# A hybrid decoder layer on Trainium2: in the first token block, norms and low parts in another order, a third projection begun early, weights divided a step ahead, and eight stores put off

## The chip, the cores and the metric

The kernel runs on one core of a Trainium2 chip. The metric is the device time of one execution in microseconds (us), and of several runs the median. A profile is one further execution, recorded by the hardware profiler. The engines are named as in the profile: PE (TensorE, matmuls and transposes), DVE (VectorE), ACT (ScalarE), POOL (GpSimd) and SP (SyncE, which issues nearly all DMA transfers here). Each engine works through its own instructions in a fixed order, and waits where an input or a buffer is not ready.

## The reference

One decoder layer over 16 meta tokens and 2048 real tokens of width 1024, in float32. Cut to what matters here:

```python
def reference(x, meta_tokens, ...):
    h = layer_norm(concatenate([meta, x], axis=1), ln_in_g, ln_in_b)
    mix = hybrid_mixer(h, w_in, b_in, ...)
    h = layer_norm(ALPHA * h + mix, ln1_g, ln1_b)
    h = layer_norm(ALPHA * h + swiglu(h), ln2_g, ln2_b)
    return h[:, N_META:]

def hybrid_mixer(h, w_in, b_in, ...):
    proj = einsum('bld,de->ble', h, w_in) + b_in
    q_s, k_s, v_s, q_g, k_g, v_g, r_g, g_lr = split(proj, cuts, axis=-1)
    o_s = sliding_window_gqa(q_s, k_s, v_s, sinks)
    o_g = chunked_gla(q_g, k_g, v_g, log_g)
    ...
    return einsum('ble,ed->bld', concatenate([o_s, o_g], axis=-1), w_out)
```

## The kernel before

**Precision.** A float32 product is made of three matmuls in a shorter format: a tile is divided into a high part (a copy on ACT, line 185) and a low part (tile minus high part, on DVE or POOL, line 186), and high x high, high x low and low x high are summed. Weights are divided once, stored to DRAM in divided form (line 226, 1024 KB each) and loaded back for later blocks (line 220).

**Tiling.** The 2048 tokens go in four blocks of 512 (`TB`), each of four tiles of 128 tokens. For each block, tokens are loaded and normalised, transposed on PE and divided into `h` (two tiles of eight 128-wide slices of the width, four each), and then multiplied by "units", blocks of 128 columns of the input projection. Unit 0 holds the window attention's keys, unit 1 its values, 2 to 5 its queries, 6 to 9 queries and keys of the gated linear attention. `project` makes one unit of one block: 24 matmuls (8 slices, 3 terms) into a PSUM bank `pu`. The first two units of the first block are begun with the first 256 tokens alone (`begin`, half-width matmuls) and finished in `project`.

**The first block.** `first_tokens` writes its order out by hand: `bank_stats`, `total`, `mean`, `square`, `variance`, `centre` and `scale` make the norm of a tile (with the power of the variance on POOL, line 422), `turn(n)` transposes tile n and divides it, `parts(u)` divides unit u. What is wrapped in `held` stays in program order on its engine. All else (matmuls of `begin`, DMA) is placed by a scheduler, which orders each engine's instructions by its own costs; so are the four blocks' further steps, listed in `WINDOW_STEPS`. `turn` also stores the divided transposed tokens to DRAM (`hT_sc`, line 461, 512 KB each, two for each tile, eight in the block), which a later stage reads.

**Buffers that set the order.** `st_u`, the staging of a unit's weights, has three buffers; `hl_u`, the divided unit, four; units 0 and 1 keep theirs until the meta tokens have been multiplied by them (`project_meta`, small matmuls `pm`). `pu` has two banks for all but the third unit. In the trace `x` is a tile of tokens, `tp` a transposed one, `kr` and `khh`/`kll` the keys, `vn`, `vd`, `vl` the values and their parts, `qraw` and `qs` queries, `s` scores, `lr` the power of a variance. Each DMA of SP also waits for the landing of the one eight places ahead of it.

**After the first block** the same steps go on for blocks 1 to 3 (divided units loaded back), then come the linear attention, the output projection and the feed-forward part.

Of the kernel before, what the change touches and what calls it, by code (L numbers as in the profile page):

```python
# [14 lines left out]
P = 128  # L15
D = 1024
KT = D // P
# [106 lines left out]
def body(ctx, tc, t, seq):  # L124
    nc = tc.nc
# [65 lines left out]

    hm = cp.tile([P, 2, KT, NM], F32R, name="hm")

    def matmuls(out, terms):
        n = len(terms)
        for i, (l, r) in enumerate(terms):
            nc.tensor.matmul(out, l, r, start=(i == 0), stop=(i == n - 1))  # L197

    rows = [slice(0, 64), slice(64, 128)]
    kTm = cp.tile([P, 2, NM], F32, name="kTm")  # L200
# [6 lines left out]
    def fetch(src, name):  # L207
        w = src.shape[1] * src.shape[2]
        st = staging(f"st_{name}")[:, :w]
        nc.sync.dma_start(st, src.rearrange("p k c -> p (k c)"))  # L210
        return st

    divided = {}

    def unit(src, name, c=P, lo_eng=None, st=None, key=None, hold=lambda i: i):

        n = src.shape[1] * src.shape[2]
        hl = wpool.tile([P, 2, D], F32R, tag="whl", name=f"hl_{name}", bufs=4)[:, :, :n]
        if key in divided:
            nc.sync.dma_start(r32(hl), divided[key])  # L220
        else:
            if st is None:
                st = fetch(src, name)
            split_into(hl[:, 0, :], hl[:, 1, :], st, lo_eng or nc.gpsimd, hold)
            divided[key] = dr.tile([P, 2, n], F32, name=f"w_{name}")
            nc.sync.dma_start(divided[key], r32(hl))
        return hl.rearrange("p a (k c) -> p a k c", c=c)


# [5 lines left out]
    def at(h, a, k):  # L235

        return h[k // 4][:, a, k % 4]
# [36 lines left out]
    with ExitStack() as c1:  # L274
# [24 lines left out]
        fetched = [fetch(t["w_u"][0], "u0_0")]  # L299
        first.append(wp.tile([P, D], F32, tag="pr", name="x_last", bufs=2))  # L300
        held(nc.sync.dma_start(first[3], t["x"][3 * P : 4 * P, :]))
        fetched.append(fetch(t["w_u"][1], "u1_0"))
        xm = wp.tile([P, D], F32, tag="pr", name="xm", bufs=2)
        nc.sync.dma_start(xm[:NM], t["meta"])
        lnt = mconst("lnt", [P, 2, KT], t["ln_in_t"])
# [86 lines left out]
            for g in range(2):  # L392
                anchor[:] = [nc.sync.dma_start(hT_sc[s][:, :, 4 * g : 4 * g + 4, q], r32(h[g])[:, :, :, q])]

        anchor = []

        def first_tokens(h):

# [27 lines left out]
            def total(n):  # L426
                sums[n] = lsmall(f"sm_{n}", [P, 1])
                held(nc.scalar.activation(junk, first[n], AF.Copy, accum_out=sums[n]))

            def mean(n):  # L430
                m[n] = lsmall(f"lm_{n}", [P, 1])
                held(nc.vector.tensor_scalar(m[n], sums[n], -1.0 / D, None, op0=ALU.mult))
# [5 lines left out]
            def variance(n):  # L438
                v[n] = lsmall(f"lv_{n}", [P, 1])
                held(nc.vector.tensor_scalar(v[n], squares[n], 1.0 / D, EPS_LN, op0=ALU.mult, op1=ALU.add))  # L440
                power(n)

            def centre(n):
                held(nc.vector.scalar_tensor_tensor(first[n], first[n], m[n], lng, op0=ALU.subtract if n == 0 else ALU.add, op1=ALU.mult))

            def scale(n):
                for g in range(2):
                    w = slice(512 * g, 512 * g + 512)
                    held(nc.vector.scalar_tensor_tensor(first[n][:, w], first[n][:, w], r[n], lnb[:, w], op0=ALU.mult, op1=ALU.add))
                nc.sync.dma_start(h_sc[n * P : n * P + P, :], first[n])  # L450

            def turn(n):
                q = slice(n * P, n * P + P)
                for g in range(2):
                    tp = t_psum(f"tp{n}_{g}") if n % 2 else s_psum(f"tp{n}_{g}").rearrange("p (k q) -> p k q", q=P)
                    for j in range(4):
                        k = 4 * g + j
                        nc.tensor.transpose(tp[:, j, :], first[n][:, k * P : (k + 1) * P], ident)
                    split_into(h[g][:, 0, :, q], h[g][:, 1, :, q], tp, None, held)
                for g in range(2):  # L460
                    stored[n] = nc.sync.dma_start(hT_sc[0][:, :, 4 * g : 4 * g + 4, q], r32(h[g])[:, :, :, q])

            w = {}

# [15 lines left out]
            turn(0)  # L480
            parts(0)
            square(2)
            centre(2)
            variance(2)
            scale(2)
            turn(1)
            begin(0, h, w[0])
            total(3)
            mean(3)
            square(3)  # L490
            centre(3)
            variance(3)
            parts(1)
            scale(3)
            turn(2)
            begin(1, h, w[1])
            turn(3)
            return stored[1], small_constants()

        halves = slice(0, TB // 2), slice(TB // 2, TB)  # L500
        EARLY_UNITS = 2
        begun = {}

        def begin(u, h, w):

            pt = mm_psum(f"pu{u}_0") if u < 2 else ps.tile([P, 512], F32, tag="L", name=f"pu{u}_0", bufs=1)
            c = halves[0]
            matmuls(pt[:, c], [m for k in range(KT) for m in ((w[:, 0, k, :], at(h, 0, k)[:, c]), (w[:, 0, k, :], at(h, 1, k)[:, c]), (w[:, 1, k, :], at(h, 0, k)[:, c]))])
            begun[u, 0] = w, pt

        def project(u, s, h, want_meta=False):
            w, pt = begun.pop((u, s), None) or (unit(t["w_u"][u], f"u{u}_{s}", P, nc.vector if (u, s) == (2, 0) else None, key=u), mm_psum(f"pu{u}_{s}"))
            terms = lambda a, b: [m for k in range(KT) for m in ((w[:, 0, k, :], a(k)), (w[:, 0, k, :], b(k)), (w[:, 1, k, :], a(k)))]
            c = halves[1] if s == 0 and u < EARLY_UNITS else slice(0, TB)
            matmuls(pt[:, c], terms(lambda k: at(h, 0, k)[:, c], lambda k: at(h, 1, k)[:, c]))
            if want_meta:
                metas[u] = w
            return pt
# [180 lines left out]
        for s in range(NSB):  # L699
            if s == NSB - 2:  # L700
                with behind(anchor):
                    tri, head, bvg, gng, eye, lev, w2, brh, brg = gla_constants()
            if s + 1 < NSB:
                hid[s + 1] = hidden(s + 1)
            for what in WINDOW_STEPS.split():
                op, k = what[0], int(what[1])
                if op == "q":
                    qs[s, k] = swa_q(s, k, hid[s])
                elif op == "S":
                    swa_scores(s, k, {c: qs.get((s, c)) for c in range(4)})  # L710
                elif op == "V":
                    swa_values(s, k)
                elif op == "G":
                    gla_qk(s, k, hid[s])
                elif s + 1 < NSB:
                    if op == "L":
                        with behind(ends if (s, k) == (0, 0) else ()):
                            load_tokens(s + 1, hid[s + 1], k)
                    elif op == "K":
                        (swa_keys, swa_vals)[k](s + 1, hid[s + 1])  # L720
                    else:
                        qs[s + 1, k] = swa_q(s + 1, k, hid[s + 1])

# [1003 lines left out]
```

## Time and profile before

| | |
|---|---|
| runs | 2231.46, 2235.39, 2230.97 us; median 2231.46 |
| the profiled execution | 2232.63 us |
| its span, first to last instruction | 2230.4 us |
| instructions | 31502 |
| mean granted clock of PE | 0.99 |
| read from and written to DRAM | 306.67 and 152.17 MB |

A row of the timeline gives start and duration in us, engine, line, operation, output and inputs, shapes and the number of merged instructions, and in brackets how long the engine had been idle and who ended that. A row of the windows gives, for each engine in turn, the us it was busy with the number of instructions, then PE's granted clock, the busy share of the DMA engines, and GB/s. A row of waits gives who waited for whom, the us in total, how often, and the longest. The page's slices are 40 equal parts of the span, with the busy share in tenths.

### The profile page before, as it was taken

What the parts mean: (1) busy time and instruction counts of PE and PEld (TensorE: products, weight loads), DVE (VectorE), ACT (ScalarE), POOL (GpSimd) and SP (SyncE); (2) the same over time, 40 slices, a digit from 0 to 9 for tenths busy, and PEclk for the clock granted to TensorE, in tenths of its full rate; (3) what the DMA queues carried; (4) which work ended last, traced back from release to release, by engine and by line L of the source; (5) the groups of instructions that cost most, each with busy time, mean ns of one, the idle gap of its engine ahead of it and who ended that gap; (6) DMA issues with size and microseconds to landing.
All of it is one profiled execution on the core that took longest, in us unless ns stands there. A gap on an engine that the chain in (4) does not pass through costs nothing.

```text
span 2230.4 us, 31502 instructions
## 1 busy us (share of the span) xinstructions
PE 2164.5 (97%) x11540; PEld 1861.3 (83%) x11540; DVE 1432.3 (64%) x2285; ACT 838.2 (38%) x1477; POOL 1219.7 (55%) x951
## 2 busy tenths in 40 slices
PE   7999999999999999999999999999999999999998
PEld 5888889888989988878888888788888888888886
DVE  6666554565745567367998666765657555865687
ACT  5555554635352343342222223222322242232343
POOL 4766545745624162258776756766666536432433
PEclk9999999999999999999999999999999999999999
DMA  9969673666676686766444317523232299655563
GB/s 328 338 225 286 226 260 114 230 258 242 239 252 262 223 319 222 297 227 223 159 166 142 112 62 259 210 85 128 81 132 81 95 345 330 216 198 170 165 232 128
DMA packets 181918, 460.92 MB, mean 207 GB/s; under 512 B 16978, under 2 KB 65011, under 8 KB 167684
## 3 DMA queue, kind: packets, MB, share of 16 engines
q1 hardware_dynamic: 176804, 452.26, 58.0%
q10 hardware_dynamic: 4960, 6.65, 0.8%
q8 instruction: 91, 1.49, 0.3%
q14 instruction: 63, 0.52, 0.1%
HBM read 306.67 MB, written 152.17 MB: 206 GB/s over the span
## 4 chain that ended last, share of the span: by engine, by line
PE 84%; DVE 6%; DMA 5%; issue 2%; POOL 2%; ACT 2%; SPq 0%; DVEq 0%; POOLq 0%; ACTq 0%
PE t L197 21%; PE d L1360 17%; PE b L197 15%; PE pu L197 11%; PE po L197 7%; PE pv L197 4%; PE lp L1134 2%; PE oa L667 2%; DMA cb<-n_scT 1%; DMA x<-x 1%; PE s L614 1%; PE s L615 1%; DMA gg<-mG_sc 1%; PE pt L655 1%; PE op L1154 1%
## 5 line engine op out<-in xcount | busy, mean ns | idle before, releaser
L1360 PE MATMUL d<-B,A 128*128 128x512 f32 x1848 | 419.3, 389 | 0.4 <-DVE A L186 0.4
L1360 PEld LDWEIGHTS d<-B,A 128*128 128x128 f32 x1848 | 346.8, 188 | 72.8 <-DVE A L186 0.8
L197 PE MATMUL t<-h_t,ps 128*128 128x512 f32 x1584 | 368.1, 390 | 5.1 <-DMA ps<-parts_ps 2.5
L197 PEld LDWEIGHTS t<-h_t,ps 128*128 128x128 f32 x1584 | 296.7, 188 | 68.1 <-ACT ps L185 2.8
L197 PE MATMUL pu<-h,hl_u 128*128 128x512 f32 (+1 forms) x1008 | 246.1, 390 | 6.4 <-ACT hl_u L185 3.3
L197 PE MATMUL b<-h_b,pa 128*128 128x512 f32 x1032 | 241.7, 389 | 0.6 <-DMA pa<-parts_pa 0.6
L197 PEld LDWEIGHTS b<-h_b,pa 128*128 128x128 f32 x1032 | 193.5, 188 | 41.2 <-issue 1.0
L186 POOL TENSOR_TENSOR pa<-a,pa 128x1024 fp32r<-128x1024 f32 x62 | 162.0, 2614 | 100.7 <-ACT pa L185 100.7
L197 PEld LDWEIGHTS pu<-h,hl_u 128*128 128x128 f32 x1008 | 180.4, 193 | 39.0 <-ACT hl_u L185 3.7
L197 PE MATMUL po<-hl_o,msh 128*128 128x256 f32 x1024 | 199.8, 291 | 3.0 <-DVE yo L913 1.5
L186 DVE TENSOR_TENSOR A<-rA,A 128x1024 fp32r<-128x1024 f32 (+1 forms) x78 | 118.8, 1549 | 122.2 <-ACT A L185 122.2
L197 PEld LDWEIGHTS po<-hl_o,msh 128*128 128x128 f32 x1024 | 164.1, 194 | 4.4 <-DVE yo L913 2.1
L185 ACT ACTIVATE A<-rA 128x1024 fp32r<-128x1024 f32 (+1 forms) x78 | 78.6, 1042 | 213.3 <-PE d L1360 199.5
L197 PE MATMUL po<-hl_o,msl 128*128 128x256 f32 x512 | 147.4, 288 | 0.0
L1630 DVE TENSOR_TENSOR u<-u,t 128x512 f32<-128x512 f32 x132 | 89.6, 681 | 82.7 <-PE t L197 82.5
L197 PE MATMUL b<-h_b,ps 128*128 128x512 f32 x528 | 125.4, 393 | 3.1 <-ACT h_b L185 2.8
L197 PE MATMUL t<-h_t,pa 128*128 128x512 f32 x528 | 123.8, 389 | 0.0
L1556 POOL TENSOR_TENSOR a<-a,a 128x1024 f32<-128x1024 f32 x42 | 121.3, 2887 | 1.6
L197 PEld LDWEIGHTS b<-h_b,ps 128*128 128x128 f32 x528 | 99.7, 189 | 25.1 <-ACT h_b L185 3.2
L197 PEld LDWEIGHTS t<-h_t,pa 128*128 128x128 f32 x528 | 99.0, 188 | 20.4
L185 ACT ACTIVATE ps<-a 128x1024 fp32r<-128x1024 f32 x63 | 66.7, 1058 | 116.6 <-PE t L197 74.8
L186 DVE TENSOR_TENSOR ps<-a,ps 128x1024 fp32r<-128x1024 f32 x42 | 77.1, 1836 | 50.2 <-ACT ps L185 47.8
(355 smaller groups left out, 4281.0 us busy)
## 6 DMA issues: line engine op xcount, KB each, us to landing
hl_u<-w_u SPq DMA_DIRECT2D x42, 1024.0 KB, 6.5
a<-w_gu SPq DMA_DIRECT2D x84, 512.0 KB, 4.7
rA<-a_sc SPq DMA_DIRECT2D x66, 512.0 KB, 4.6
w<-w_d SPq DMA_DIRECT2D x50, 512.0 KB, 5.4
hl_o<-w_o SPq DMA_DIRECT2D x24, 1024.0 KB, 7.2
hT_sc<-h SPq DMA_DIRECT2D x32, 512.0 KB, 6.6
gh<-hT_sc SPq DMA_DIRECT2D x16, 1024.0 KB, 9.6
w_u<-hl_u SPq DMA_DIRECT2D x14, 1024.0 KB, 8.3
```

The source lines that it names most:

```text
L185: hold(nc.scalar.activation(hi, src, AF.Copy))
L186: hold((lo_eng or nc.vector).tensor_tensor(lo, src, r32(hi), op=ALU.subtract))
L197: nc.tensor.matmul(out, l, r, start=(i == 0), stop=(i == n - 1))
L614: nc.tensor.matmul(sp[:, :272], q, khh[:, hh, w], start=True, stop=False)
L615: nc.tensor.matmul(sp[:, :272], q, kll[:, hh, w], start=False, stop=True)
L655: nc.tensor.transpose(tp[:, x, :], pr[:, n, 2 * (x % 2) + x // 2, NM:144], ident)
L667: nc.tensor.matmul(oa[:, n], l, m, start=False, stop=(hh == 1 and i == 5))
L1134: nc.tensor.matmul(o[:, P * j : P * j + P], kl[:, j, :], x[:, :, j, :], start=True, stop=True)
L1154: nc.tensor.matmul(op[:, P * h : P * h + P], am[:, h, :], vg[n][:, 16 + P * h : 16 + P * h + P], start=False, stop=(h % 2 == 1))
L1360: nc.tensor.matmul(pt, a_[:, a, ca], fb[:, b, cb], start=(p == 0 and j == 0), stop=(p == NP - 1 and j == 2))
L1556: sub = lambda o, x, y: nc.gpsimd.tensor_tensor(o, x, y, op=ALU.subtract)
L1630: nc.vector.tensor_tensor(o[i], x[i], y[i], op=ALU.add)
```

## The change

- The low parts of a token tile are placed directly behind its high parts: tile 1 is turned ahead of the centring of tile 2, and unit 1's parts come ahead of the square of tile 3.
- A third unit is fetched at the start, divided in `first_tokens` and begun with the first 256 tokens (in another PSUM tile, `L`); its second half is 24 half-width matmuls in `project`. The matmuls of the begun units' second halves are kept in program order.
- Weights are divided a step ahead: at the end of `project` of a unit of the first block, the next unit's division is begun (`ahead`, order in `FIRST_UNITS`).
- The eight stores of `hT_sc` for the first block are collected (`put_off`) and issued at the end of the block's steps, behind the store of the last divided unit.

```diff
-    def matmuls(out, terms):
+    def matmuls(out, terms, hold=lambda i: i):
...
-            nc.tensor.matmul(out, l, r, start=(i == 0), stop=(i == n - 1))
+            last = hold(nc.tensor.matmul(out, l, r, start=(i == 0), stop=(i == n - 1)))
+        return last
...
-            nc.sync.dma_start(divided[key], r32(hl))
+            stored_parts.append(nc.sync.dma_start(divided[key], r32(hl)))
...
-        fetched.append(fetch(t["w_u"][1], "u1_0"))
+        fetched += [fetch(t["w_u"][u], f"u{u}_0") for u in (1, 2)]
...
-                    stored[n] = nc.sync.dma_start(hT_sc[0][:, :, 4 * g : 4 * g + 4, q], r32(h[g])[:, :, :, q])
+                    put_off.append((hT_sc[0][:, :, 4 * g : 4 * g + 4, q], r32(h[g])[:, :, :, q]))
...
             turn(0)
             parts(0)
             square(2)
-            centre(2)
-            variance(2)
-            scale(2)
             turn(1)
             begin(0, h, w[0])
             total(3)
+            centre(2)
+            variance(2)
             mean(3)
+            parts(1)
             square(3)
+            scale(2)
+            begin(1, h, w[1])
+            variance(3)
             centre(3)
-            variance(3)
-            parts(1)
             scale(3)
             turn(2)
-            begin(1, h, w[1])
+            parts(2)
             turn(3)
+            begin(2, h, w[2])
+            ahead(3, 0, held)
...
-        EARLY_UNITS = 2
+        EARLY_UNITS = 3
...
+        FIRST_UNITS = [3, 6, 5, 4, 9, 8, 7]
+        units_ahead = {}
+
+        def ahead(u, s, hold=lambda i: i):
+            units_ahead[u, s] = unit(t["w_u"][u], f"u{u}_{s}", P, None, key=u, hold=hold)
...
-            w, pt = begun.pop((u, s), None) or (unit(t["w_u"][u], f"u{u}_{s}", P, nc.vector if (u, s) == (2, 0) else None, key=u), mm_psum(f"pu{u}_{s}"))
+            w, pt = begun.pop((u, s), None) or (units_ahead.pop((u, s), None) or unit(t["w_u"][u], f"u{u}_{s}", P, None, key=u), mm_psum(f"pu{u}_{s}"))
...
+            if s == 0 and u in FIRST_UNITS[:-1]:
+                ahead(FIRST_UNITS[FIRST_UNITS.index(u) + 1], 0)
...
+            if s == 0:
+                with behind(stored_parts[-1:]):
+                    for o, x in put_off:
+                        nc.sync.dma_start(o, x)
```

What this makes of the instructions' order is seen at three places.

**PE, at the start.** `tp` are the transposes of the token tiles (`x_215` is tile 2, `x_last` tile 3), `pu` the units. Before, `pu_0_346` is unit 0, `pu_0_406` unit 1, `pu_0_559` unit 2:

```order
L197 MATMUL pu_0_346<-h_0_257,hl_u_0_315 128x256
L458 MATMUL tp_0_390<-ident,x_215 128x128 x4
L458 MATMUL tp_1_397<-ident,x_215 128x128 x4
L197 MATMUL pu_0_346<-h_0_257,hl_u_0_315 128x256 x11
L197 MATMUL pu_0_346<-h_1_258,hl_u_0_315 128x256 x12
L197 MATMUL pu_0_406<-h_0_257,hl_u_0_382 128x256 x12
L197 MATMUL pu_0_406<-h_1_258,hl_u_0_382 128x256 x12
L458 MATMUL tp_0_431<-ident,x_last 128x128 x4
L458 MATMUL tp_1_438<-ident,x_last 128x128 x4
```

Now `pu_0_336` is unit 0, `pu_0_380` unit 1, `pu_0_446` unit 2:

```order
L197 MATMUL pu_0_336<-h_0_259,hl_u_0_315 128x256 x12
L197 MATMUL pu_0_336<-h_1_260,hl_u_0_315 128x256 x12
L197 MATMUL pu_0_380<-h_0_259,hl_u_0_370 128x256 x12
L197 MATMUL pu_0_380<-h_1_260,hl_u_0_370 128x256 x12
L459 MATMUL tp_0_413<-ident,x_215 128x128 x4
L459 MATMUL tp_1_420<-ident,x_215 128x128 x4
L459 MATMUL tp_0_432<-ident,x_last 128x128 x4
L459 MATMUL tp_1_439<-ident,x_last 128x128 x4
L197 MATMUL pu_0_446<-h_0_259,hl_u_0_427 128x256 x12
L197 MATMUL pu_0_446<-h_1_260,hl_u_0_427 128x256 x12
```

Units 0 and 1 are begun ahead of the transposes of tiles 2 and 3, and unit 2 is begun behind them; the second halves of units 0, 1 and 2 and then unit 3 follow.

**POOL, behind the first part of the block.** `x_726` and `x_986` (before), `x_749` and `x_1009` (now) are the first two tiles of the next block, `hl_u_0_691` (before) and `hl_u_0_639` (now) unit 6, `hl_u_0_886` and `hl_u_0_739` unit 5. Before:

```order
L172 TENSOR_TENSOR lr_in_995<-lv_in_993,neghalf 128x1
L383 TENSOR_TENSOR x_726<-x_726,lnb 128x512 x2
L564 TENSOR_TENSOR vd_516<-vlast,vn_515 128x128
L565 TENSOR_TENSOR vd_516<-vn_515 128x384
L186 TENSOR_TENSOR vl<-vn_515,vh 128x4x2x64
L382 TENSOR_TENSOR x_986<-x_986,lng 128x512
L383 TENSOR_TENSOR x_986<-x_986,lnb 128x512
L186 TENSOR_TENSOR hl_u_0_691<-st_u_0_692,hl_u_0_691 128x1024
L595 TENSOR_TENSOR qs_0_585<-qraw_0_584,qs_0_585 64x512 x2
```

And now, with PE's rows of the same place (`pu_0_714` is unit 6, `pu_0_909` unit 5, `pu_0_1079` unit 4) behind it:

```order
L172 TENSOR_TENSOR lr_in_1018<-lv_in_1016,neghalf 128x1
L384 TENSOR_TENSOR x_749<-x_749,lnb 128x512 x2
L186 TENSOR_TENSOR hl_u_0_639<-st_u_0_640,hl_u_0_639 128x1024
L383 TENSOR_TENSOR x_1009<-x_1009,lng 128x512
L384 TENSOR_TENSOR x_1009<-x_1009,lnb 128x512
L577 TENSOR_TENSOR vd_547<-vlast,vn_546 128x128
L578 TENSOR_TENSOR vd_547<-vn_546 128x384
L186 TENSOR_TENSOR vl<-vn_546,vh 128x4x2x64
L384 TENSOR_TENSOR x_1009<-x_1009,lnb 128x512
L608 TENSOR_TENSOR qs_0_608<-qraw_0_607,qs_0_608 64x512 x2
```

```order
L197 MATMUL pu_0_714<-h_1_260,hl_u_0_639 128x512 x6
L391 MATMUL tp_0_768<-ident,x_749 128x128 x4
L197 MATMUL pu_0_909<-h_0_259,hl_u_0_739 128x512 x2
L197 MATMUL pu_0_1079<-h_0_259,hl_u_0_934 128x512 x2
L391 MATMUL tp_1_775<-ident,x_749 128x128 x4
```

The low part of unit 6 has moved ahead of `vd`, `vl` and two instructions for the next tile. On PE unit 6 is now finished ahead of the first transposes of the next block, and the first two matmuls of units 5 and 4 stand behind them; before, two matmuls of unit 6, then two of unit 5, stood ahead of the rest of unit 6. On ACT the order behind the second query (`qs` of unit 3) is now: high part of unit 4, copy of unit 6 (`gr`), high part of unit 9, half a token tile.

**SP, from the first stores on.** `h_sc<-x` stores a normalised tile, `hT_sc_149` is the store that the change puts off, `w_u<-hl_u` the store of a divided unit, `st_u<-w_u` a fetch of weights. Before:

```order
L450 DMA h_sc<-x_210 128x1024
L450 DMA h_sc<-x_212 128x1024
L461 DMA hT_sc_149<-h_0_257 256x4x128
L461 DMA hT_sc_149<-h_1_258 256x4x128
L226 DMA w_u_0_318<-hl_u_0_315 128x2048
L210 DMA st_u_0_592<-w_u 128x1024
L450 DMA h_sc<-x_215 128x1024
L461 DMA hT_sc_149<-h_0_257 256x4x128
L461 DMA hT_sc_149<-h_1_258 256x4x128
L284 DMA x_726<-x 128x1024
L284 DMA x_986<-x 128x1024
L226 DMA w_u_0_385<-hl_u_0_382 128x2048
```

And now:

```order
L451 DMA h_sc<-x_210 128x1024
L451 DMA h_sc<-x_212 128x1024
L285 DMA x_749<-x 128x1024
L227 DMA w_u_0_318<-hl_u_0_315 128x2048
L211 DMA st_u_0_472<-w_u 128x1024
L285 DMA x_1009<-x 128x1024
L227 DMA w_u_0_373<-hl_u_0_370 128x2048
L211 DMA st_u_0_640<-w_u 128x1024
L451 DMA h_sc<-x_215 128x1024
L451 DMA h_sc<-x_last 128x1024
L227 DMA w_u_0_430<-hl_u_0_427 128x2048
L211 DMA st_u_0_740<-w_u 128x1024
```

The load of the next block's first tile (`x_749`) now stands directly behind the stores of the first two tiles; it takes the buffer of the first, so SP waits there for that store to land. The eight stores of `hT_sc_149` stand 31 places further on, behind the store of unit 7, and ahead of the load that brings unit 2 back for block 1.

More of the change, by code (lines that the diff above doesn't have):

```diff
@@ L211, in fetch @@
         return st
-    divided = {}
+    divided, stored_parts = {}, []
     def unit(src, name, c=P, lo_eng=None, st=None, key=None, hold=lambda i: i):
@@ L393, in load_tokens @@
                 anchor[:] = [nc.sync.dma_start(hT_sc[s][:, :, 4 * g : 4 * g + 4, q], r32(h[g])[:, :, :, q])]
-        anchor = []
+        anchor, put_off, last_matmul = [], [], []
         def first_tokens(h):
@@ L449, in scale @@
                     held(nc.vector.scalar_tensor_tensor(first[n][:, w], first[n][:, w], r[n], lnb[:, w], op0=ALU.mult, op1=ALU.add))
-                nc.sync.dma_start(h_sc[n * P : n * P + P, :], first[n])
+                stored[n] = nc.sync.dma_start(h_sc[n * P : n * P + P, :], first[n])
             def turn(n):
@@ L507, in begin @@
             c = halves[0]
-            matmuls(pt[:, c], [m for k in range(KT) for m in ((w[:, 0, k, :], at(h, 0, k)[:, c]), (w[:, 0, k, :], at(h, 1, k)[:, c]), (w[:, 1, k, :], at(h, 0, k)[:, c]))])
+            matmuls(pt[:, c], [m for k in range(KT) for m in ((w[:, 0, k, :], at(h, 0, k)[:, c]), (w[:, 0, k, :], at(h, 1, k)[:, c]), (w[:, 1, k, :], at(h, 0, k)[:, c]))], held if u == 2 else lambda i: i)
             begun[u, 0] = w, pt
+        FIRST_UNITS = [3, 6, 5, 4, 9, 8, 7]
+        units_ahead = {}
+        def ahead(u, s, hold=lambda i: i):
+            units_ahead[u, s] = unit(t["w_u"][u], f"u{u}_{s}", P, None, key=u, hold=hold)
         def project(u, s, h, want_meta=False):
-            w, pt = begun.pop((u, s), None) or (unit(t["w_u"][u], f"u{u}_{s}", P, nc.vector if (u, s) == (2, 0) else None, key=u), mm_psum(f"pu{u}_{s}"))
+            w, pt = begun.pop((u, s), None) or (units_ahead.pop((u, s), None) or unit(t["w_u"][u], f"u{u}_{s}", P, None, key=u), mm_psum(f"pu{u}_{s}"))
             terms = lambda a, b: [m for k in range(KT) for m in ((w[:, 0, k, :], a(k)), (w[:, 0, k, :], b(k)), (w[:, 1, k, :], a(k)))]
             c = halves[1] if s == 0 and u < EARLY_UNITS else slice(0, TB)
-            matmuls(pt[:, c], terms(lambda k: at(h, 0, k)[:, c], lambda k: at(h, 1, k)[:, c]))
+            last_matmul[:] = [matmuls(pt[:, c], terms(lambda k: at(h, 0, k)[:, c], lambda k: at(h, 1, k)[:, c]), held if s == 0 and u < 2 else lambda i: i)]
+            if s == 0 and u in FIRST_UNITS[:-1]:
+                ahead(FIRST_UNITS[FIRST_UNITS.index(u) + 1], 0)
             if want_meta:
```

## The prediction

> **What bounds the kernel now.** I read the page first, then what TensorE (PE) waited for in the first 60 us, then single stretches of the timeline there.
>
> ```profile
> span 2230.4 us, 31502 instructions
> PE 2164.5 (97%) x11540; PEld 1861.3 (83%) x11540; DVE 1432.3 (64%) x2285; ACT 838.2 (38%) x1477; POOL 1219.7 (55%) x951
> PE   7999999999999999999999999999999999999998
> DMA  9969673666676686766444317523232299655563
> ```
>
> PE is busy in every slice but the first. The change touches the first block of 512 tokens, so it can win only what PE loses there. That loss is in the waits of the first 60 us:
>
> ```profile
> PE tp L458 <- DVE x L449: 4.0, 2, 2.8
> PE tp L458 <- issue: 3.5, 1, 3.5
> PE pu L197 <- ACT hl_u L185: 3.3, 1, 3.3
> PE bc L404 <- DMA row_g<-ln_in_g: 2.8, 1, 2.8
> PE pu L197 <- ACT h L185: 2.1, 2, 1.6
> ```
>
> With three small ones (0.5, 0.2, 0.2) they make 16.6 us. The first load (2.8) and the first norm (3.5, and 1.1 of the 4.0) stand ahead of the change, so about 9 us are in reach. PE's timeline (start, time, count, in brackets the wait ahead) shows where:
>
> ```profile
> 15.62 0.58 PE L197 MATMUL pu<-h,hl_u 128*128 128x256 f32 x1 [0.51 <-ACT h L185]
> 19.02 1.94 PE L458 MATMUL tp<-ident,x 128*128 128x128 f32 x8 [2.82 <-DVE x L449]
> 20.61 7.13 PE L197 MATMUL pu<-h,hl_u 128*128 128x256 f32 x47
> 27.58 1.03 PE L458 MATMUL tp<-ident,x_last 128*128 128x128 f32 x8
> 30.93 10.87 PE L197 MATMUL pu<-h,hl_u 128*128 128x256 f32 x67 [0.22 <-DVE h L186]
> 42.75 6.42 PE L197 MATMUL pu<-h,hl_u 128*128 128x512 f32 x27
> 52.30 0.72 PE L197 MATMUL pu<-h,hl_u 128*128 128x512 f32 x2 [0.49 <-ACT qs L594]
> 56.31 7.94 PE L197 MATMUL pu<-h,hl_u 128*128 128x512 f32 x24 [3.29 <-ACT hl_u L185]
> 66.23 0.37 PE L614 MATMUL s<-khh,qs 128*128 128x272 f32 x1
> 69.12 4.15 PE L197 MATMUL pu<-h,hl_u 128*128 128x512 f32 x17
> ```
>
> There are two holes, one before 20.61 and one before 56.31. The 24 matmuls at 56.31 take 331 ns each against 238 in the row above, because the clock is halved; the windows (PEclk is the number ahead of the last two) show it, and again behind a wait of 2.58 us that ended at 200.56:
>
> ```profile
> 54.00:56.00 2.00, 0.00 (x0) 0.00 (x0) 0.00 (x0) 1.95 (x3) 2.00 (x2) 0.55 1.13 346
> 60.00:62.00 2.00, 2.00 (x8) 1.63 (x7) 1.80 (x2) 0.92 (x4) 1.95 (x2) 0.75 0.92 246
> 200.56 0.36 PE L614 MATMUL s<-khh,qs 128*128 128x272 f32 x1 [2.58 <-DVE mx L617]
> 202.00:204.00 2.00, 2.00 (x7) 1.56 (x7) 1.20 (x7) 0.81 (x2) 0.90 (x2) 0.50 1.02 314
> ```
>
> The 0.75 of the third row is half slow, half fast, so from 56.31 to 61.0 PE works at half speed: 2.35 us lost.
>
> **Step 1, up to the fourth unit.** The prices of high parts (ACT) and low parts (DVE) are the medians of these rows, in ns, for weights and for half a token tile:
>
> ```profile
> L185 ACT ACTIVATE hl_u<-st_u x10: 1042/1054/1062, 12.5 to 87.0; 128x1024 fp32r<-128x1024 f32 x10
> L186 DVE TENSOR_TENSOR hl_u<-st_u,hl_u x3: 1215/1220/1221, 14.9 to 27.6; 128x1024 fp32r<-128x1024 f32 x3
> L185 ACT ACTIVATE h<-tp x16: 574/587/600, 11.2 to 108.7; 128x512 fp32r<-128x512 f32 x16
> L186 DVE TENSOR_TENSOR h<-tp,h x16: 677/684/693, 13.7 to 109.4; 128x512 fp32r<-128x512 f32 x16
> ```
>
> Now low parts of token tile 1 come straight behind the high ones, so the first 24 matmuls need not wait for the norm of tile 2. DVE ends the low part of unit 0 at 14.9 + 1.2 = 16.1 (unchanged), two low parts of a token tile follow, so PE flows from about 16.7, not 20.6. At 152 ns (7.13/47, half clock at first) to 215 (if the clock stays halved) 24 end at 20.4 to 21.9. Unit 1 follows (its low part is done near 20), to 23.9 to 25.4. Two groups of transposes take 1.03 each. ACT then needs some 3.2 for two tiles (two halves of 0.53, start to start) and unit 2, with DVE 1.5 behind it (near 29.2), and the third unit's 24 end at 30.7 to 32.1. The other 72 half-width matmuls cost 128 ns each: of the 67 at 30.93, 21 are full width at 238 ns, which leaves 5.87/46. That makes 9.2, then 24 full ones 5.7 and the eleven small transposes 1.1 more: 47 to 48.1. Before, this point was 49.17 (42.75 + 6.42). **Step 1 is worth 1 to 2 us**; the 24 additional matmuls (48 x 0.128 for 24 x 0.238, 0.4 us) are inside it. The additional fetch (512 KB) goes ahead of small constants whose first user is DVE, behind 29 us. SP now waits for a first store of h before the load of the next tokens, some 5 us from 15.6 on, and the fetch of unit 3 stands behind it, near 21.5; without the four stores of h in its way it still lands by 28.
>
> **Step 2, the chain on POOL and ACT.** Behind unit 3 it is not PE that decides but low parts made on POOL, and the query parts on ACT:
>
> ```profile
> 37.32 1.29 DVE L166 BATCH_NORM_STATS2 st_in<-x 128x6 f32<-128x512 f32 x2 [2.51 <-DMA x<-x]
> 45.29 0.93 POOL L172 TENSOR_TENSOR lr_in<-lv_in,neghalf 128x1 f32<-128x1 f32 x1 [2.47 <-DVE lv_in L170]
> 46.19 2.59 POOL L383 TENSOR_TENSOR x<-x,lnb 128x512 f32<-128x512 f32 x2
> 50.62 1.26 POOL L186 TENSOR_TENSOR vl<-vn,vh 128x512 fp32r<-128x512 f32 x1
> 51.84 1.27 POOL L382 TENSOR_TENSOR x<-x,lng 128x512 f32<-128x512 f32 x1
> 53.08 1.26 POOL L383 TENSOR_TENSOR x<-x,lnb 128x512 f32<-128x512 f32 x1
> 54.31 2.34 POOL L186 TENSOR_TENSOR hl_u<-st_u,hl_u 128x1024 fp32r<-128x1024 f32 x1
> 53.61 1.56 ACT L594 ACTIVATE qs<-pu,bq,slp 64x512 fp32r<-64x512 f32 x2
> 55.20 1.06 ACT L185 ACTIVATE hl_u<-st_u 128x1024 fp32r<-128x1024 f32 x1
> 64.74 7.07 POOL L186 TENSOR_TENSOR hl_u<-st_u,hl_u 128x1024 fp32r<-128x1024 f32 x3
> ```
>
> POOL works without a break from 45.29 to 71.8. Its start hangs on DVE, and DVE at 37.32 on tokens 512 to 639, whose load stood behind the eight stores' first four. Without them the load is early, and DVE goes on behind the meta tokens' norm at about 33.1. So POOL's chain starts 3.9 us earlier (between 3 and 4.2, the whole of DVE's gain). In it unit 6's low part now follows the row at 46.19 at once, ahead of the two vd, vl and the two for x: these took from 48.78 to 54.31, 5.5 us. It ends at 54.31 + 2.34 - 3.9 - 5.5 = 47.2, when PE gets there. Unit 6's 24 (5.7) and sixteen small meta matmuls (1.8: from 64.4, behind the 24 and four transposes, to 66.23) run through, to about 54.5.
>
> But vl is now behind 2.34 + 1.27 + 1.26: it ends at 51.88 - 3.9 + 4.87 = 52.85, and ACT's second query waits for it. 0.7 (qraw, 52.94 to 53.61) + 1.56 later, at 55.2, PE gets the bank for unit 5's first two; unit 4's first two need the copy of unit 6 (0.7, as the query's), behind unit 4's high part: 55.2 + 1.05 + 0.7 = 56.9. The second group of transposes needs ACT's unit 9 and half tile (1.05 + 0.6) and DVE's 0.69: 59.3. With 0.45 and 1.8 for meta matmuls unit 5 goes on at **61.6**, where it went on at 69.12. Stores of 1024 KB and loads are not late for this: SP is free earlier. Work that stood ahead of 69.12 and now stands behind (one group of transposes 0.45, eight score matmuls 1.1, two small ones 0.4) is 1.95. So 69.12 - 61.6 - 1.95 = **5.5 us earlier**, step 1 included (4 if POOL wins only 3 and PE is late by 0.6; 6.5 if unit 9's 1.05 on ACT is not in the way of the half tile). PE's waits there are now 0.7, 1.4 and 1.9 us: 4 in sum, as long as the 3.8 (3.29 + 0.49) they replace.
>
> **Step 3, the clock.** Between 54.5 and 61.6 PE does 0.9 us of transposes, four large matmuls and sixteen tiny ones. In before, two full-speed matmuls and some tiny ones did not keep the clock up, and at 200.56 a hole of 2.58 sufficed. I take it that the clock is halved again, for as much dense work as before: 2.4 us, between 0 and 3.4. Here a page speaks against me: the Trainium skill, "TensorE: Matmul & The Clock Gate", section "HAM oscillation — how this bites in real kernels", asks only that there be no idle gap above some 3.4 us. By it 0.7, 1.4 and 1.9 would be harmless; the wait of 2.58 at 200.56, with 0.50 behind it, does not bear it out.
>
> **Step 4, the eight stores.** They leave the stretch of 16 to 54 us and come behind the last divided weight, near 80 us. The same bytes are moved by 108 us, in another order, while the queue is full:
>
> ```profile
> 80.00:100.00 20.00, 20.00 (x109) 17.28 (x109) 12.17 (x40) 11.61 (x30) 17.46 (x13) 1.00 1.00 358
> 102.38 0.32 SPq L220 DMA_DIRECT2D hl_u<-w_u x1
> 112.28 4.60 PE L197 MATMUL pu<-h,hl_u 128*128 128x512 f32 x19
> ```
>
> Eight times 0.524 MB at 358 GB/s are 11.7 us. The first thing behind them that PE needs is the reload of unit 2 for the second block, issued at 102.38 and used from 112.28 (now about 109). I cost it at nothing: what is put off was taken out earlier, and the page's DMA row falls from 9 to 6 in its third slice (111 to 167 us), which leaves room behind. Bounds: 0 and 10 us.
>
> **Sum.** 5.5 - 2.4 = 3.1 us less. Behind 66 us PE is the bound, so that it stays, give or take the waits further on. The scheduler orders the later blocks anew, too; the wait at 200.56 with its slow clock (2.58 + 1.7) shows what such a place is worth, either way, and I leave it at zero. The profiled execution took 2232.63 (its span 2230.4 and 2.2 around it), 1.2 over the median of the three runs, 2231.46. So 2229.5 against the one, and **2228.4** against the median. A measurement tells about 0.2% (4.5 us) from no change, so 2227.0 and 2235.9 are the bounds.
>
> **Rivals.**
> - The clock stays up, or falls for one short stretch: 5.5 to 6 us less, **2225.7**. For it: three short waits in place of one long. Against it: 200.56. Chance 0.27.
> - Nothing arrives: the time won comes back in later waits, since the order of block 1 and after is new, or the third projection's early half only fills a hole in front of the same chain. For it: vl, moved back, puts ACT's second query at the 55.2 that it had. Against it: POOL's other parts are 4 to 9 us earlier. **2231.5**, chance 0.18.
> - The put-off stores collide with the reload of unit 2. For it: they stand ahead of it on SP, and SP, now waiting for landings and for POOL, leaves the queue empty for some us that the old order used. If all 11.7 us come on top, the reload lands at 108.1 + 11.7 = 119.8 instead of by 109.2: 10.6 late, **2239**. It decides the sign from a landing 3.1 us behind 109.2 on. Against it: the bytes are the same. Chance 0.13.
>
> **Numbers.** Forecast 0.42, rivals 0.27, 0.18, 0.13. The low end is the clock rival with the wait of 200.56 gone, 2222; the high end a reload some 6 us late, 2235. Faster by over 0.2%: 0.27 and a fifth of the forecast (order), 0.36. Slower: 0.14. Within: 0.50.
>
> **What would show it.** Step 1: no matmul of tiles 0 and 1 behind 25.5 us; unit 3 done at 47 to 48. Step 2: POOL's lr_in for token tile 5 near 41.4, unit 6's low part before vd, unit 5 going on near 61.6, PE's waits named qs, gr and h. Step 3: PEclk near 0.5 somewhere in 56 to 66. Step 4: no PE wait on hl_u<-w_u in 100 to 125. It would be wrong if unit 3's weights land after 29 us, if the wait on the first store of h holds SP beyond 22 us, or if a PE wait above 2 us appears between 66 and 250 that was not there.

## The result, and the profile after

The changed kernel takes **2218.61 us** (median of six runs, 2216.87 to 2222.30) against 2231.69 before: a ratio of 0.9937, with a 95% interval of 0.9923 to 0.9951. It is faster by 13 us by the medians, 11 to 17 by the interval; 3 were forecast, and the low end of the range was 2222. The page of the changed kernel, in the lines that answer to those of before:

```profile
span 2215.0 us, 31559 instructions
PE 2158.8 (97%) x11564; PEld 1858.7 (84%) x11564; DVE 1444.7 (65%) x2285; ACT 838.1 (38%) x1477; POOL 1220.2 (55%) x951
PE   8899999999999999999999999999999999999998
DMA  8987773576786787766352318523232299655463
```

The span is 15.4 us shorter, with 24 matmuls more. Where PE won them is read from the windows, by stage (width, then busy us of PE, PEld, DVE, ACT and POOL, then PEclk). Before:

```profile
0.00:100.00 100.00, 83.21 (x436) 69.41 (x437) 62.55 (x143) 56.10 (x98) 60.38 (x54) 0.97 0.99 340
100.00:300.00 200.00, 195.05 (x1133) 169.73 (x1132) 119.93 (x372) 104.17 (x276) 118.53 (x102) 0.99 0.79 259
300.00:505.00 205.00, 198.16 (x1274) 176.96 (x1272) 109.97 (x306) 97.67 (x254) 111.39 (x146) 0.98 0.57 200
505.00:800.00 295.00, 286.35 (x2069) 269.70 (x2070) 161.03 (x359) 120.20 (x257) 122.33 (x216) 0.98 0.70 251
800.00:1010.00 210.00, 195.21 (x1318) 177.93 (x1317) 128.50 (x232) 79.19 (x146) 93.46 (x101) 0.98 0.72 260
```

And the changed kernel:

```profile
0.00:100.00 100.00, 86.59 (x446) 72.94 (x447) 63.55 (x132) 55.62 (x96) 60.09 (x54) 0.93 0.86 309
100.00:300.00 200.00, 193.27 (x1136) 169.49 (x1135) 120.74 (x374) 103.81 (x276) 117.32 (x100) 0.99 0.84 274
300.00:505.00 205.00, 196.81 (x1280) 175.03 (x1279) 111.81 (x311) 96.32 (x246) 114.02 (x147) 1.00 0.56 200
505.00:800.00 295.00, 293.80 (x2140) 276.56 (x2139) 176.25 (x384) 129.33 (x278) 136.58 (x244) 1.00 0.74 269
800.00:1010.00 210.00, 196.33 (x1315) 178.83 (x1314) 131.05 (x220) 74.42 (x138) 92.28 (x79) 0.98 0.72 260
```

Width less PE's busy time is idle; width times (1 - PEclk) is what half clock costs at most (PE is also idle in it), to the rounding of PEclk. In the first 100 us idle falls from 16.8 to 13.4, but the clock's share rises from 3 to 7: nothing is won where the change was made. The experiments below leave more profiles of the same two first blocks, and idle and half clock together are 17 to 20 us with before's (x2, x5, x6, x11, x12 and before itself) and 20 to 21 with the changed one (x1, x3 and the changed kernel itself). From 100 to 300 idle rises by 1.8; from 300 to 505 it rises by 1.35, while the half clock there (0.98) goes, some 4 us. **From 505 to 800 us idle falls from 8.65 to 1.2 and the clock's loss from some 6 (in narrower windows 5) to nothing: 12 to 13 us**, in a stage that no line of the diff touches, the linear attention with the output projection of the block before it. What differs there is the order of its instructions: on PE 2734 of 8960 instructions stand at another place than before, though they were written in the same order.

### The profile page after: what moved, and what is told of

Its sections match the earlier page's. It is cut to its first block, busy times and chain, and to the rows that moved or that the text cites. A ratio compares the mean times of both kernels' runs of the same rounds, so it can differ in the third digit from the quotient of the medians.

```text
span 2215.0 us, 31559 instructions
## 1 busy us (share of the span) xinstructions
PE 2158.8 (97%) x11564; PEld 1858.7 (84%) x11564; DVE 1444.7 (65%) x2285; ACT 838.1 (38%) x1477; POOL 1220.2 (55%) x951
## 4 chain that ended last, share of the span: by engine, by line
PE 85%; DMA 4%; DVE 4%; POOL 3%; issue 2%; ACT 2%; SPq 0%; DVEq 0%; POOLq 0%; ACTq 0%
PE t L197 20%; PE d L1377 18%; PE b L197 14%; PE pu L197 13%; PE po L197 6%; PE pv L197 4%; PE lp L1151 2%; PE oa L680 1%; DMA r_t<-t_sc 1%; DMA cb<-n_scT 1%; DMA x<-x 1%; PE s L627 1%; PE s L628 1%; ACT pr L643 1%; PE nt L943 1%
## 5 line engine op out<-in xcount | busy, mean ns | idle before, releaser
L185 ACT ACTIVATE pa<-a 128x1024 fp32r<-128x1024 f32 x62 | 65.8, 1060 | 110.1 <-PE t L197 52.7
## 6 DMA issues: line engine op xcount, KB each, us to landing
gh<-hT_sc SPq DMA_DIRECT2D x16, 1024.0 KB, 10.5
```

Of the source, the lines that this page charges most:

```text
L185: hold(nc.scalar.activation(hi, src, AF.Copy))
```

## The experiments

Everything from the second block on (15148 instructions) is written alike in both kernels. So the scheduler's order of one can be imposed on the other, by edges of order alone between neighbours on each engine; places come from a table:

```diff
+def in_order(tc, n):
+    tail = list(tc.nc.cur_bb.bb.instructions)[-n:]
+    for o in ORDERS:
...
+        for a, b in zip(o, o[1:]):
+            tc.add_manual_dep(tail[b], tail[a].name, DependencyInfo(NoSync, DATA), reason="order")
...
             body(ctx, tc, t, seq)
+            in_order(tc, 15148)
```

Ratios below are to runs of before on the same chip, with their 95% intervals. "Before's kind" and "the changed kind" is the order of the linear stage.

**Whose order, whose first block.** x1: changed first block, before's later order.

> The changed kernel, with everything that is written for blocks 1 to 3 and behind (15148 instructions, each engine) held in the order in which the kernel before has it; the first block's instructions stand as in the changed kernel. Theory A (the 13 us come from the order that the scheduler gave the later stages, above all 500 to 800 us, and the first block by itself is no better, since PE has lost 26 us to waits and half clock by 130 us where it had lost 21): about 2236 us, between 2231 and 2241, and the half-clock stretches near 395, 460, 559 and 645 us are back. Theory B (the first block's change makes the gain, and what follows only passes it on): about 2219 us. The forecast on record (3 us from the first block, nothing from the order): 2228.

2247.28 us, 1.0058 (1.0037 to 1.0079): slower than before, so theory B falls. Theory A has the sign; the time is 6 us above its range. x2 is the reverse:

> The kernel before, with everything written for blocks 1 to 3 and behind held in the order in which the changed kernel has it; the first block stands as before. Theory A: about 2213 us (2209 to 2219): the later order brings its 14 to 20 us without the changed first block, and PE shows hardly a wait between 510 and 800 us. Theory B: about 2232 us.

**2214.59 us, 0.9907 (0.9888 to 0.9927)**: the gain without any of the first block's change. One row of each (505 to 800 us, columns as above), x1 first:

```profile
505.00:800.00 295.00, 286.66 (x2087) 270.29 (x2086) 162.46 (x366) 118.93 (x262) 113.82 (x199) 0.98 0.69 246
```

```profile
505.00:800.00 295.00, 294.46 (x2148) 277.48 (x2147) 177.39 (x381) 129.35 (x271) 137.93 (x249) 1.00 0.74 272
```

The idle time (8.3 and 0.5 us) and the half clock go with the order, not with the first block. x3 is the control, the changed kernel with its own order held:

> Control: the changed kernel with its own later order held by the same means; every engine's order is the changed kernel's, instruction for instruction. If holding an order costs nothing by itself: 0.993 to 0.995 of before, about 2219 us.

2221.22 us, 0.9942 (0.9925 to 0.9958): holding costs nothing that shows. x5 and x6 divide the order in two: the linear stage with all behind it, and the window attention.

> The kernel before: first block and the window attention of blocks 1 to 3 in its own order; only what is written for the linear attention and behind it (the last 12970 instructions) is held in the order of the changed kernel. If the gain sits in the order of that stage (PE waits 9.5 us between 505 and 800 us in before, 1.1 in the changed kernel, and 5 us of half clock there against none): about 2219 us, between 2215 and 2224. If it sits in the order of the window attention, or needs both: 2228 to 2233.

2217.56 us, 0.9921 (0.9902 to 0.9941): the linear stage's order alone, in an otherwise unchanged kernel, is worth 15 us by the medians, 13 to 22 by the interval.

```profile
505.00:800.00 295.00, 294.00 (x2139) 276.89 (x2140) 175.93 (x381) 129.37 (x272) 137.19 (x246) 1.00 0.75 271
```

> The counterpart: the kernel before with only the window attention of blocks 1 to 3 (2178 instructions) held in the changed kernel's order. If the gain sits in the linear stage's order: about 2229 us (the 3 us that PE loses less between 200 and 400), between 2224 and 2234, with the waits of 505 to 800 us as before. If in the window attention's: about 2219.

2227.96 us, 0.9973 (0.9960 to 0.9987): some 5 us, as expected. The two parts, 15 and 5, make up x2's 19.

**The stores.** y1 and f3 are one edit, with the later order held (changed kind) and free:

```diff
-                with behind(stored_parts[-1:]):
+                with behind([stored_parts[-1], stored_gr[0, 3]]):
```

> The changed kernel (later order held as in it), but the eight put-off stores also come behind the store of unit 9's output (gqk_sc<-gr), which in the changed kernel stands behind seven of them and holds the single gr buffer. Theory C (the new PE wait of 3.4 us at 111.9, the 0.66 ahead of it and 1.7 of half clock come from that store's place in SP's queue): about 2213 us, and no PE wait on gr above 1 us near 112. Rival D (the stores are only in the way of something else a little later, the reload of unit 2 or the next gr store): about 2218 us, with a wait of the same size in 110 to 130.

2217.45 us, 0.9923 (0.9906 to 0.9941). The wait on gr near 112 is gone, as theory C has it, but the time is not its 2213, and the whole can't be told from the changed kernel's.

> The changed kernel with the eight stores also behind the store of unit 9's output, as in y1, but now the scheduler orders everything after it anew. Its order of the linear attention comes out near that of the kernel before (273 of 8960 places on PE differ from before, 2728 from the changed kernel). If the order of that stage makes the gain: 2217 and the 10 to 12 us of that stage, about 2228 us, between 2224 and 2234, although the code is the changed kernel's but for the place of eight stores. If the changed first block makes the gain: about 2217, as y1.

2242.22 us, 1.0035 (1.0020 to 1.0050). Moving eight stores by some places turned the linear stage back to before's kind, and the gain was gone; the time is 8 us above the range that I gave, so the kind is not all that got worse (idle from 100 to 300 us is 7.5, in y1 3.4).

z1, z2 and f1 are before with the stores alone put off; its later order held as before's, held as the changed kernel's, and free.

> The kernel before (later order held as in it), with the eight stores of hT_sc put off as in the change and nothing else. If their leaving the first 54 us lets POOL's chain start 4 us earlier, as forecast, PE's wait of 3.3 us for unit 6 and the half clock behind it (2.4) go: about 2226 us. If the stores collide near 100 us with the outputs' stores, as theory C has it, 4 to 6 us come back there: about 2231 us. No later order changes, so by theory A nothing near 2219 is to be had here.

2253.60 us, 1.0094 (1.0071 to 1.0117), far outside both theories. PE's busy time in 100 to 300 us falls to:

```profile
100.00:300.00 200.00, 180.79 (x1017) 156.89 (x1016) 106.92 (x339) 96.27 (x251) 108.93 (x93) 0.95 0.75 242
```

That is 19 us idle, in an order that was made with the stores elsewhere; f1 below tells what that is worth.

> The kernel before with only the eight stores put off, as z1 (which took 20 us more than before), but the later order is held as in the changed kernel; to be read against x2 (before's first block, this later order, stores not put off: 2214.6). If the 20 us come from a later order that was made for other transfer times: about 2217 us, as the same stores cost the changed kernel little. If putting off these stores costs 20 us by itself behind before's first block: about 2234 us.

2234.33 us, 0.9997 (0.9984 to 1.0011): 16.2 us idle between 100 and 300, 1.1 between 505 and 800. The first theory's 2217 missed; the second has the number, but f1 takes its reason away:

> The kernel before with only the eight stores put off, nothing held: the scheduler makes the later order for it, and its linear stage is of before's kind. If z1's 20 us came from an order that did not fit the new transfer times: 2230 to 2240 us, with the waits of before in 505 to 800 us (about 9 us). If putting off these stores costs 20 us by itself: about 2253.

2235.64 us, 1.0016 (1.0004 to 1.0027): with an order made for it, putting off costs some 3.5 us; the rest of z1's loss came with the held order ("misfit" from here on).

**The other parts.** In e3 and f2 the stores stand where before has them (`nc.sync.dma_start` in `turn`); in p3 and f4 both calls of `ahead` are left out; p2 and f5 have both edits. e3, p3 and p2 hold the changed kernel's later order, f2, f4 and f5 are free.

> The changed kernel, its later order held, but the eight stores of hT_sc issued in the first block where they were before, not put off. If the put-off stores cost the 5 us seen at 106 to 115 us and bring little in the first 60: about 2214 us, and no PE wait on gr near 112. If their leaving the first 54 us brings the 3 to 4 us forecast: about 2218 us, with the low part of unit 6 late by as much.

2223.85 us, 0.9947 (0.9928 to 0.9967). The longest of PE's waits in its first 130 us, as total, count and longest:

```profile
PE pu L215 <- ACT hl_u L203: 5.4, 2, 4.6
```

A wait of 4.6 us for unit 6 is there and none on gr is left. The time is above both theories, and the ratio can't be told from x3's 0.9942: the stores cost at one end about what they bring at the other.

> The changed kernel with the eight stores where they were before, nothing held; linear stage of before's kind. If the kind of order decides: no faster than before, 2230 to 2240 us. If the changed first block brings the gain: 2219 to 2224, as e3, which has the same first block and the changed kernel's later order.

2244.82 us, 1.0054 (1.0038 to 1.0071): e3's first block in before's kind of order, 5 us above the range.

> The changed kernel, later order held, without the division of weights a step ahead. By the forecast (step 2: unit 6's low part early on POOL ends the hole ahead of unit 6, 3.3 us and 2.4 of half clock) its loss costs up to 5 us: 2220 to 2224. If the scheduler places the divisions early anyway (nearly the same order stands on ACT and POOL): within 2 us of the changed kernel, 2217 to 2221.

2235.69 us, 1.0006 (0.9993 to 1.0019), outside both: 16.2 us idle between 100 and 300. The next run, with an order of its own, has 7.8, so this is another misfit.

> The changed kernel without the division a step ahead, nothing held; its linear stage is of the changed kernel's kind. If the kind of order decides, and p3's 15 us came from a window-attention order that did not fit: about 2220 us, between 2214 and 2226, with under 2 us of PE waits in 505 to 800 us. If the division ahead is needed for the gain: 2232 to 2236, as p3.

2227.90 us, 0.9980 (0.9969 to 0.9991): faster than before, 2 us above the range; 2.6 us idle in 505 to 800, where under 2 of waits were expected.

> The changed kernel, later order held, with neither the division ahead nor the stores put off: of the first block's change only the order of norms and low parts and the third projection are left. Against x2 (nothing of the first block's change: 2214.6) it tells what these two are worth: by the forecast (step 1) 1 to 2 us less, 2213; if the earlier start of the third projection is paid for in half clock and in late weights of unit 6 (e3, with the division ahead: 2223.9, with a PE wait of 4.6 us for unit 6): 2220 to 2226.

2230.68 us, 0.9989 (0.9977 to 1.0000): above the range; not the 1 to 2 us less than x2 that step 1 forecast. Idle from 100 to 300 us is 11.6, and how much of that is misfit isn't separated.

> Of the first block's change only the order of norms and low parts and the third projection, nothing held; linear stage of before's kind (40 of 8960 places differ). If the kind of order decides: no faster than before, 2230 to 2238 us. If these two edits bring what step 1 forecast and no more: about 2230 too, so this run speaks only against a gain of 10 us from them.

2250.69 us, 1.0075 (1.0058 to 1.0093): the sign is right, the time 13 us above the range. These two edits alone, in an order made for them, cost some 17 us by the ratio; why so much isn't shown.

**Which part of the linear stage.** x11 and x12 exchange 593 neighbouring matmuls. Only PE's order of the linear stage is held in them; the other engines follow.

> The kernel before; of the linear stage only 593 matmuls on PE in one piece (output projection of block 0 and chunks 4 to 7 of the linear attention) are in the changed kernel's order, all others on PE as before (the other engines follow). If the products lp that wait for xq make the loss there: the 3.6 us of waits and 3.4 of half clock in 505 to 600 us go, about 2225 us (2222 to 2229), and the wait for the reload at 670 us stays. If the gain needs the order as a whole: 2230 to 2234.

2228.60 us, 0.9973 (0.9961 to 0.9985), in the range of the first theory. The waits on xq are gone from 505 to 600, where before shows the first two rows, but x11 has a new one:

```profile
PE lp L1134 <- DVE xq L1129: 4.1, 4, 1.5
PE lp L1142 <- DVE amat L1140: 0.4, 1, 0.4
```

```profile
PE ot L1192 <- ACT ogn L1189: 2.0, 1, 2.0
```

> The counterpart: the linear stage in the changed kernel's order on PE but for those 593 matmuls, which stand as before. By the first theory the 7 us of 505 to 600 us are back and the rest of x5's gain stays: about 2225 us (2221 to 2229), without a wait for the reload near 660 us. If the piece has no part in it: 2217 as x5.

2224.82 us, 0.9960 (0.9947 to 0.9973), in the range of the first theory; but from 505 to 600 only idle time is back (5.0 us), not the half clock. The two pieces bring 4.6 and 8.4 us, 13 together, of x5's 15: the gain is spread over the stage, with about a third of it in the first piece.

**All in one table** (idle of PE in us, from the windows):

| kernel | first block | linear stage | ratio | idle 100-300 | idle 505-800 |
|---|---|---|---|---|---|
| before | before | before's kind | 1 | 5.0 | 8.7 |
| x6 | before | before's, held | 0.9973 | 3.2 | 7.9 |
| f1 | stores put off | before's, free | 1.0016 | 9.7 | 7.7 |
| f3 | changed, stores later | before's, free | 1.0035 | 7.5 | 8.2 |
| f2 | changed, stores early | before's, free | 1.0054 | 9.4 | 8.4 |
| x1 | changed | before's, held | 1.0058 | 9.9 | 8.3 |
| f5 | norms, third unit | before's, free | 1.0075 | 10.5 | 7.8 |
| z1 | stores put off | before's, held | 1.0094 | 19.2 | 7.3 |
| x11 | before | before's but for 593 | 0.9973 | 5.1 | 7.1 |
| x12 | before | changed but for 593 | 0.9960 | 5.5 | 6.5 |
| x2 | before | changed, held | 0.9907 | 3.8 | 0.5 |
| x5 | before | changed, held | 0.9921 | 5.4 | 1.0 |
| y1 | changed, stores later | changed, held | 0.9923 | 3.4 | 0.7 |
| the changed kernel | changed | changed, free | 0.9937 | 6.7 | 1.2 |
| x3 | changed | changed, held | 0.9942 | 6.5 | 1.4 |
| e3 | changed, stores early | changed, held | 0.9947 | 5.5 | 1.3 |
| f4 | no ahead | changed, free | 0.9980 | 7.8 | 2.6 |
| p2 | norms, third unit | changed, held | 0.9989 | 11.6 | 1.2 |
| z2 | stores put off | changed, held | 0.9997 | 16.2 | 1.1 |
| p3 | no ahead | changed, held | 1.0006 | 16.2 | 1.2 |

But for x11 and x12, which mix the two orders, the last column has two values only, 7 to 9 and 0.5 to 2.6, and the kind of order sets which. Four first blocks stand on both sides (x1 and the changed kernel, f3 and y1, f2 and e3, f5 and p2): the kind is worth 0.9 to 1.2% in each, 19 to 27 us, with whatever differs in the window attention's order and with misfit where an order is held. Within a kind no changed first block is ahead of before's own; y1 comes level with x5. x2 is the fastest of all, though its interval still touches the changed kernel's.

## Why the prediction was wrong

**The step that failed** is the one sentence in the sum: "The scheduler orders the later blocks anew, too; ... and I leave it at zero." It was worth 15 us (x5), and 19 with the window attention's order (x2). The same error stands at the start: "it can win only what PE loses there", in the first block. I took the later order for noise of a few us around one mean. It is not: two kinds were found, and the change landed in the other one. That the time moved the way I forecast is luck: f2, f3 and f5, which carry much of the same change, are slower than before. One place shows how the order works. In before, DVE's xq takes 2.07 us in place of 0.42, beside a low part on POOL; PE has two matmuls of the output projection (`po`) to do and then waits 1.47 us (DVE, POOL, then PE's rows):

```profile
557.83 2.07 DVE L1129 TENSOR_TENSOR xq<-e,gqh 128x256 f32<-128x256 f32 x1 [0.47 <-PE lp L1134]
...
557.27 2.34 POOL L186 TENSOR_TENSOR hl_o<-st_o,hl_o 128x1024 fp32r<-128x1024 f32 x1 [1.99 <-ACT hl_o L185]
...
557.08 0.71 PE L1134 MATMUL lp<-xq,gqk 128*128 128x128 f32 x4 [1.15 <-DVE xq L1129]
...
557.99 0.36 PE L197 MATMUL po<-hl_o,msh 128*128 128x256 f32 x1
558.20 0.28 PE L197 MATMUL po<-hl_o,msl 128*128 128x256 f32 x1
559.95 1.22 PE L1134 MATMUL lp<-xq,e 128*128 128x128 f32 x4 [1.47 <-DVE xq L1129]
```

In the changed kernel the same thing takes DVE as long, but PE has the output projection to do meanwhile and doesn't wait:

```profile
565.72 2.02 DVE L1146 TENSOR_TENSOR xq<-e,gqh 128x256 f32<-128x256 f32 x1
...
566.38 0.48 PE L197 MATMUL po<-hl_o,msh 128*128 128x256 f32 x2
...
568.01 1.05 PE L1151 MATMUL lp<-xq,e 128*128 128x128 f32 x8
```

The order on PE around these products, with the number of matmuls as written (one of `lp` shows as four in the timeline), first before's, then the changed kernel's:

```
po0_0_1 12, sp4 2, lp4_4 2, lp4_2 2, lp4_6 2, lp4_4 2, po0_0_1 2, lp5_0 2, lp4_6 2
po0_0_1 2, lp4_4 2, lp4_2 2, po0_0_1 17, po0_1_1 11, lp4_6 2, lp4_4 2, po0_1_1 13, po0_2_1 7, lp5_0 2, po0_2_1 7, lp4_6 2
```

Before, the products of a chunk follow one another; in the changed kernel 7 to 28 matmuls of the projection stand between them. This place is a part of it only (x11). What tips the scheduler from one kind to the other isn't settled: of the kernels left free, before, f1, f2, f3 and f5 have the one, the changed kernel and f4 the other, and f3 and the changed kernel differ only in where eight stores are issued. Counted in places on PE, f1, f2, f3 and f5 stand 40 to 273 of 8960 from before, f4 467 from the changed kernel, and the two kinds some 2700 from each other.

**Step 1** (1 to 2 us) brought 0.3. PE's timeline of the changed kernel, with the rows that the next points need too:

```profile
17.09 8.39 PE L197 MATMUL pu<-h,hl_u 128*128 128x256 f32 x47 [0.59 <-DVE h L186]
28.03 0.51 PE L197 MATMUL pu<-h,hl_u 128*128 128x256 f32 x2 [0.81 <-ACT hl_u L185]
29.29 16.46 PE L197 MATMUL pu<-h,hl_u 128*128 128x256 f32 x109 [0.75 <-DVE hl_u L186]
46.72 6.42 PE L197 MATMUL pu<-h,hl_u 128*128 128x512 f32 x27
58.60 0.74 PE L197 MATMUL pu<-h,hl_u 128*128 128x512 f32 x2 [1.06 <-ACT gr L692]
60.76 1.12 PE L391 MATMUL tp<-ident,x 128*128 128x128 f32 x4 [1.42 <-DVE h L186]
64.94 1.20 PE L197 MATMUL pu<-h,hl_u 128*128 128x512 f32 x2
67.68 4.69 PE L197 MATMUL pu<-h,hl_u 128*128 128x512 f32 x14
111.86 6.03 PE L197 MATMUL pu<-h,hl_u 128*128 128x512 f32 x19 [3.41 <-ACT gr L692]
```

PE did flow from 17.1, and tiles 0 and 1 were done by 25.5, as forecast. But the third unit waited for its high and its low part, and behind these two waits the clock was halved, which step 1 had not counted. That loss comes and goes: in x1, with the same two waits, PEclk is 1.00 from 30 to 32, and with before's first block it is 0.50 from 32 to 34 in x2 and x5. Of the 27 matmuls at 46.72 nine end unit 3: at 48.9, before 49.2.

```profile
30.00:32.00 2.00, 2.00 (x12) 2.00 (x10) 2.00 (x2) 0.00 (x0) 2.00 (x1) 0.50 1.04 422
60.00:70.00 10.00, 8.77 (x32) 7.78 (x33) 9.43 (x16) 2.03 (x7) 9.25 (x6) 0.52 0.84 274
112.00:114.00 2.00, 2.00 (x5) 1.61 (x6) 1.76 (x6) 0.00 (x0) 2.00 (x2) 0.50 1.12 365
```

**Step 2** had the chain right and its times too early. Without the stores DVE came to tokens 512 to 639 at 35.03 and not at 33.1, so POOL's chain started 2.4 us earlier than before (42.86 for 45.29), less than the 3 that I gave as its least. Unit 6's low part on POOL ran ahead of vd and ended at 49.2 (47.2 forecast), still in time for PE; ACT's second query ended at 56.8 (55.2 forecast). POOL's and ACT's rows:

```profile
42.86 1.00 POOL L172 TENSOR_TENSOR lr_in<-lv_in,neghalf 128x1 f32<-128x1 f32 x1
...
46.32 2.84 POOL L186 TENSOR_TENSOR hl_u<-st_u,hl_u 128x1024 fp32r<-128x1024 f32 x1
...
55.20 1.56 ACT L607 ACTIVATE qs<-pu,bq,slp 64x512 fp32r<-64x512 f32 x2
```

PE waited on gr (1.06) and h (1.42), as named; the wait on qs was hidden behind unit 6. Unit 4's first two matmuls came at 58.60 (56.9 forecast) and the transposes at 60.76 (59.3), so the chain was 1.5 to 1.7 us late; unit 5 went on at 64.94 and 67.68 in place of 61.6.

**Step 3** was mis-sized, and with it unit 5's place: the clock was halved for nearly all of 60 to 70. PE was busy for 8.77 us of it, so 4.2 us were lost by that row (8.77 times 0.48) where I took 2.4, and the sixteen matmuls of the meta tokens took 3.4 us (61.53 to 64.94) in place of 1.8. The Trainium skill, "TensorE: Matmul & The Clock Gate", section "HAM oscillation — how this bites in real kernels", would have let waits of 1.06 and 1.42 us pass; the row does not agree. So in 100 us of this pair of profiles the first block won 3.4 us of idle time and gave 4 back to the clock.

**Step 4** (nothing; the rival: a collision with the reload of unit 2) was wrong in its place. Seven stores hold SP for 13.6 us, and behind them stands the store of unit 9's output:

```profile
86.92 13.59 SPq L739 DMA_DIRECT2D hT_sc<-h  x7
100.61 1.49 SPq L693 DMA_DIRECT2D gqk_sc<-gr  x1
```

The issues themselves last up to 4.1 us each (90.37 to 94.44); the transfer eight places ahead had landed before each of them began, so it is not that wait, and what holds them isn't shown.
There is one buffer gr: the next copy out of PSUM must wait for that store to land, 6.5 us behind its issue (at 107.1), and stands on ACT behind eight exponentials besides, so that it comes at 111.1. PE waits 3.41, with half clock behind it (row of 112 to 114): the wait above 2 us between 66 and 250 that I had named as a sign of being wrong. y1 takes both away: there the copy runs at 96.7, ahead of the exponentials. The reload of unit 2 made no wait, as forecast. The stores' cost and their use in the first 54 us are about equal (e3).

**The rivals.** "The clock stays up" fell. "Nothing arrives" is nearest the truth for the first block; its further reason, that the order of later blocks is new, named the right place and had the wrong sign. The range held neither, since its ends moved the first block's terms only.

## What to carry to other kernels

Where a scheduler orders the whole program, an edit at its start changes the order of everything behind it, and that may be worth more than the edit: compare the orders stage by stage before costing the edit, and give a stage whose order changed a term and a spread of its own. To learn what an edit is worth, measure it with the later order held and also free: an order made for one first block cost another some 18 us (z1 against f1), so neither alone is the answer. The gain here is the order of the later stages, above all the linear one (x2, x5), and it can be had by holding that order, without the change.

## What the runs showed of the hardware

A two-input DVE operation of 0.42 us took 2.07 and 2.02 us where it began 0.6 to 0.7 us behind a low part on POOL, and ended 0.3 us after it (before: POOL's 557.27 and 2.34, DVE's 557.83 and 2.07; the changed kernel: POOL's 565.06 and 2.39, DVE's 565.72 and 2.02). The Trainium skill, "SBUF — State Buffer", section "Who interferes with whom", says that such an operation is kept out wholly by a POOL instruction that reads SBUF and began earlier; the trace agrees here. The clock was halved for some 10 us at waits of 1.06 and 1.42 us in a stretch of small matmuls (0.52 from 60 to 70), and again in x1 (0.51 from 62 to 72) and y1 (0.50 from 59 to 69) at the same waits. At two waits of 0.81 and 0.75 us it was halved in the changed kernel (0.50 from 30 to 32) and not in x1 (1.00), so these waits alone don't decide it.
